# Another order of the input products and other ranks in a planned hybrid encoder block

## The chip, the cores and the metric

The kernel runs on one core of a Trainium2 chip. Its time is the device time of one execution in microseconds (us), the median over several runs; lower is better. The engines that count here are TensorE (PE, with its weight loads PEld), VectorE (DVE), ScalarE (ACT), GpSimd (POOL) and the queue from which all transfers are issued (SP). TensorE's products are the bulk of the work.

## The reference, cut to what matters

One encoder block over 1024 positions of width 1024, eight heads of 128, everything in float32:

```python
h = rms_norm(x, g_mix)
proj = h @ w_in          # glu_a, glu_b | q, k, v | z | decay and beta logits | gate_a, gate_b
c = glu_a * sigmoid(glu_b)
c = depthwise_conv(c, conv_dw_w) + conv_dw_b            # 31 taps
y_conv = silu(layer_norm(c)) @ w_conv_out
q, k, v = silu(depthwise_conv([q, k, v], qkv_conv_w))   # 5 taps, then q and k to unit length
o = rms_norm(gated_delta_rule(q, k, v, ...) + reversed one) * silu(z)
y_delta = o @ w_delta_out
x = x + (sigmoid(gate_a) * y_conv + sigmoid(gate_b) * y_delta) @ w_o
...                                     # SwiGLU, the per-layer embedding, the last norm
```

The change touches the time in which the first four groups of lines are computed, a little over the first half of the run.

## The kernel before, in words

**Products.** A float32 product is made of three products of rounded parts: `mm3` multiplies a high and a low part of the weights with a high and a low part of the activations. One block of 128 output columns needs 24 such products over 512 positions for each half of the positions (in the profile `ps<-big,w 128x512`, called *big products* here). Its weights come by DMA (`raw`), are rounded to the high part on ACT (a cast, `w<-raw`) and subtracted to the low part on DVE (`w<-raw,w`).

**The blocks.** `MAIN` and `FILL` list the blocks of the input projection by a letter and a number: `q`, `k`, `v` (with a 5-tap convolution and SiLU, head by head), `l` (the logits), `g` (a GLU pair, followed on DVE by the 31 taps of its convolution, `conv31`), `z` (the output gate), `a` and `b` (the two branch gates), `p` (the projection of the per-layer input). After them come `conv_out` (the layer norm, named `ln` below, and the product `cout` with `w_conv_out`), and four calls of `group`, the delta rule for two heads each. Later come `dout` (the product with `w_delta_out`, from the stored outputs `d_o` of the heads) and everything else.

**The delta rule.** For two heads, `group` turns k and q (`transpose`, with squares on ACT for their lengths), loads decay rows from DRAM (`big<-dg`) to which ACT adds a bias eight times, forms matrices, and inverts 32 by 32 blocks on DVE (30 pairs of small operations). `head` then joins blocks to 64 and to 128 (`d.lev`: a product `ps<-big`, a negating copy on ACT to a tile `m`, a product `ps<-big,m`, copies of its result on ACT, two STREAM_TRANSPOSE on DVE, and the same once more), and walks along eight chunks in both directions (`d.chain`: products with the state `S`, with `xin` from DVE, with `z2` from ACT). One head follows the other, and other products fill the gaps.

**The order.** Nothing is issued in the order of the code. `Plan` records all operations, and `order` places them by a list schedule with costs of its own: each operation has a rank and a number in the order of recording, and of those that are ready the lowest pair goes first. Tiles are handed out in the order of recording for each line of use.

```python
o.key = (self.level, o.idx)                     # add: rank, then order of recording
pn.level = LV["w"] if 1 <= lv < 3 else lv       # load_w: weights go ahead of their block
if c.key[0] > o.key[0] + 0.6 or ...             # order, on ACT: no table switch for a near rank
w[1][0] < o.key[0] - 0.5                        # order, on DVE: hold a long operation back
```

`LV` holds the ranks: `w` weights, `delta` the delta rule, `qkv`, `glu`, `z` the blocks, `conv31` the taps, `gate` the branch gates, `ln` and `cout` the end of the convolution branch. What follows (`dout` and later) has rank 1. The order is fixed when the kernel is built; on the chip each engine takes its own list in order and waits where an input is late.

Of the kernel before, what the change touches and what calls it, by code (L numbers as in the profile page):

```python
# [565 lines left out]
def cs(j):  # L566
# [2 lines left out]


N_BIG, N_MID, N_W, N_D = 32, 8, 6, 11
LV = dict(w=-3.0, logits=-0.2, delta=-1.8, qkv=1.3, glu=1.2, z=0.5, conv31=2.7, gate=2.3, pl=-0.3, ln=2.1, cout=2.4)
CAP = dict(raw5=6, acc5=3, cpad=10, acc31=1, lnev=3, wmain=4, wfill=2, bank=2, x0=4)
LEAD = (1, 3, 3)
PAIRS = (3, 3, 3)
# [18 lines left out]

MAIN = ("k0 q0 v0 l0 g0 z0 k1 q1 z2 v1 g1 z1 q3 k2 g2 v3 v2 q2 k3 k4 q4 z3 z4 a4 k5 g3 v5 z6 v4 g4 "
        "v6 q5 k7 q6 a5 g5 a7 k6 z5 z7 g6 v7 g7 a6 q7")
FILL = "a0 a2 a3 a1 b0 b1 b2 b3 p0 b4 b5 b6 b7"
PL_AFTER = 2  # L600


def ORDER(f):
# [3 lines left out]
          "a": lambda i: f["do_gate"](0, i), "b": lambda i: f["do_gate"](1, i)}  # L607
    for w in (MAIN + " " + FILL).split():
        do[w[0]](int(w[1:]))
# [5 lines left out]
def hybrid_block(tc, x, p, g_mix, w_in, conv_dw_w, conv_dw_b,  # L615
# [13 lines left out]
    def to(level, stream, sec=None):  # L629
        pn.level, pn.stream, pn.sec = level, stream, sec or stream  # L630

    def large(shape=None, dtype=F32, line="t", cap=99):
        return big.tile(shape or [P, T], dtype, tag="big", line=line, cap=cap)

    def medium(shape=None, dtype=F32, line="ev", cap=4, stream=None):
        return mid.tile(shape or [P, HW], dtype, tag="mid", line=line, cap=cap, stream=stream)
# [65 lines left out]
    def load_w(w, r0, nk, c0, cap=4, pool=None):  # L702

        lv, parts = pn.level, []
        st = "main" if pn.stream == "main" else "rest"
        pn.level = LV["w"] if 1 <= lv < 3 else lv
        for k0 in range(0, nk, 4):
# [135 lines left out]
    def logits():  # L843
        to(LV["logits"], "logits")
        wr = medium([P, KB, 32], line="wab")
# [47 lines left out]
    def load_cols(c0, cap=CAP["wmain"]):  # L893
        return load_w(w_in[0], 0, KB, c0, cap)
# [17 lines left out]
    def do_qkv(which, hd):  # L912
        to(LV["qkv"], "main", "qkv")
        b = which * NH + hd
        w = first_w.pop() if first_w else load_cols(C_Q + b * P)
        raw = large([P, T + SK - 1], line="raw5", cap=CAP["raw5"])
        for h in range(2):
            ps = block_half(w, hA, h, KB)
            pn.act(raw[:, 2 + h * HW:2 + (h + 1) * HW], ps)
        pn.fill(raw[:, 0:2], 0.0)  # L920
        pn.fill(raw[:, T + 2:T + 4], 0.0)
        acc = large(line="acc5", cap=CAP["acc5"])
        conv(acc, raw, cw5[:, b], SK)
        pn.act(acc, acc, AF.Silu)
        pn.dma(d_qkv[which][hd], acc)
# [3 lines left out]
    def do_glu(b):  # L929
        to(LV["glu"], "main", "glu")  # L930
        wb = load_cols(C_GLUB + b * P)
        sg = [ev2(), ev2()]
        for h in range(2):
            pn.act(sg[h], block_half(wb, hA, h, KB), AF.Sigmoid)
        wa = load_cols(C_GLUA + b * P)
        c = large([P, T + CK - 1], line="cpad", cap=CAP["cpad"])
        for h in range(2):
            pa = block_half(wa, hA, h, KB)
            pn.tt(c[:, 15 + h * HW:15 + (h + 1) * HW], pa, sg[h], ALU.mult)
        pn.fill(c[:, 0:15], 0.0)  # L940
        pn.fill(c[:, T + 15:T + 30], 0.0)
        to(LV["conv31"], "conv31")
        acc = large(line="acc31", cap=CAP["acc31"])
        conv(acc, c, cw31[:, b], CK, bias=col["cb31"][:, b:b + 1])
        for h in range(2):
            pn.dma(d_y[b][h], acc[:, hs(h)])
        if b == 0:
            pn.copy(lnacc, acc)
        else:
            pn.tt(lnacc, lnacc, acc, ALU.add)  # L950

    def do_gate(i, b):
        to(LV["gate"], "fill", "gate")
        w = load_cols((C_GA, C_GB)[i] + b * P, CAP["wfill"])
        for h in range(2):
            ps = block_half(w, hA, h, KB)
            sg = ev2()
            pn.act(sg, ps)
            pn.dma(d_gate[i][b][h], sg)
# [954 lines left out]
```

## Time and profile before

| | |
|---|---|
| median of 3 runs | 2108.96 us (2108.37 to 2110.83) |
| the profiled execution: its own time | 2112.86 us |
| its span, first to last instruction | 2111.1 us |
| PE busy | 2071.5 us, 98% |
| DVE busy | 1639.3 us, 78% |
| ACT busy | 1143.8 us, 54% |
| mean granted TensorE clock | 0.994 |

PE is the engine to read: it is nearly always busy, so that the time is what its instructions take, plus the moments in which it waits for another engine or a transfer, plus what a lower granted clock adds. Idle time of DVE or ACT costs nothing by itself. "Who waited for whom" is listed by releaser: an instruction that waits for several things is put down to the last one.

### The profile page before, as it was taken

Reading aid. Unit: us, or ns where it says so; the run is one execution under the profiler, and the core shown is the slowest. Engines: PE = TensorE matmul, PEld = TensorE weight load, DVE = VectorE, ACT = ScalarE, POOL = GpSimd, SP = SyncE. Lnnn points to the kernel's source line nnn. Section 1 sums busy time; section 2 is a strip of 40 time slices with the busy share of each in tenths; the row PEclk is TensorE's granted clock in tenths of the full one; section 3 lists DMA queues with packets and bytes.
Section 4 is the critical chain, followed back from the end, with each engine's and each line's share of the span. In section 5 each row is a group of like instructions: output and inputs, shape, how many; then the busy total and the mean of one; then the engine's idle time right before and its main releaser. Section 6 shows DMA issues by size and latency. Waiting matters only on the chain.

```text
span 2111.1 us, 29502 instructions
## 1 busy us (share of the span) xinstructions
PE 2071.5 (98%) x10279; PEld 1701.3 (81%) x10279; DVE 1639.3 (78%) x2683; ACT 1143.8 (54%) x2603; POOL 129.1 (6%) x197
## 2 busy tenths in 40 slices
PE   8999999999999999999999999999999999999998
PEld 6888888788888788878877788887777777777888
DVE  5578969877999899996687767787666657888776
ACT  6726674657766664857875444433333335443542
POOL 1000111011200211001100000000000000000000
PEclk9999999999999999999999999999999999999999
DMA  6334332533333421544567686433333337442253
GB/s 220 126 102 134 106 118 68 179 95 111 135 101 115 140 83 68 199 149 161 165 206 234 204 278 209 127 120 105 100 96 104 100 99 264 154 160 80 66 161 104
DMA packets 296726, 292.85 MB, mean 139 GB/s; under 512 B 17945, under 2 KB 217810, under 8 KB 296576
## 3 DMA queue, kind: packets, MB, share of 16 engines
q1 hardware_dynamic: 296576, 290.95, 42.8%
q8 instruction: 81, 1.33, 0.3%
q14 instruction: 69, 0.57, 0.1%
HBM read 205.10 MB, written 85.79 MB: 138 GB/s over the span
## 4 chain that ended last, share of the span: by engine, by line
PE 64%; DVE 6%; ACT 4%; issue 1%; DMA 1%; POOL 0%; DVEq 0%; SPq 0%; POOLq 0%; ACTq 0%
PE ps L243 63%; DVE big L291 4%; ACT big L268 2%; PE ps L248 1%; DVE mid L291 1%; DVE w L291 1%; ACT big L275 1%; ACT w L268 0%; ACT m L275 0%; DMA raw<-in_w_delta_out_dram 0%; ACT mid L268 0%; POOL rn L320 0%; DMA mid<-d 0%; DMA big<-dqkv 0%; DMA big<-dg 0%
## 5 line engine op out<-in xcount | busy, mean ns | idle before, releaser
L243 PE MATMUL ps<-big,w 128*128 128x512 f32 (+1 forms) x7416 | 1825.7, 400 | 5.7 <-ACT w L268 3.9
L243 PEld LDWEIGHTS ps<-big,w 128*128 128x128 f32 x7416 | 1360.2, 189 | 316.6 <-ACT w L268 5.8
L291 DVE SCALAR_TENSOR_TENSOR big<-big,cw 128x1024 f32<-128x1024 f32 x336 | 433.5, 1295 | 17.3 <-ACT big L275 11.2
L268 ACT CAST w<-raw 128x512 fp32r<-128x512 f32 (+2 forms) x308 | 185.5, 607 | 275.0 <-PE ps L243 225.8
L291 DVE TENSOR_TENSOR w<-raw,w 128x512 fp32r<-128x512 f32 (+2 forms) x308 | 208.9, 681 | 85.9 <-ACT w L268 83.1
L268 ACT CAST w<-mid 128x512 fp32r<-128x512 f32 (+1 forms) x185 | 108.3, 588 | 153.6 <-PE ps L243 121.9
L291 DVE TENSOR_TENSOR big<-big 128x512 fp32r<-128x512 f32 (+2 forms) x238 | 161.5, 702 | 12.0 <-ACT big L268 8.4
L291 DVE TENSOR_TENSOR w<-mid,w 128x512 fp32r<-128x512 f32 (+1 forms) x185 | 118.7, 644 | 60.3 <-ACT w L268 59.4
L291 DVE TENSOR_TENSOR big<-ps,big 128x512 f32<-128x512 f32 (+1 forms) x146 | 99.9, 687 | 36.6 <-PE ps L243 27.2
L268 ACT CAST big<-big 128x512 fp32r<-128x512 f32 x163 | 96.2, 622 | 43.7 <-DVE big L291 23.3
L268 ACT COPY big<-big 32x128 f32<-32x128 f32 (+1 forms) x264 | 103.1, 441 | 18.7 <-DVE big L291 16.8
L243 PE MATMUL ps<-big 128*128 128x128 f32 (+1 forms) x784 | 104.6, 280 | 7.8 <-ACT big L268 5.1
L243 PEld LDWEIGHTS ps<-big 128*128 128x128 f32 x784 | 98.9, 191 | 16.4 <-issue 11.2
L268 ACT COPY big<-ps 128x512 f32<-128x512 f32 (+3 forms) x178 | 74.9, 429 | 65.3 <-PE ps L243 56.2
L275 ACT ACTIVATE mid<-mid 128x512 f32<-128x512 f32 (+2 forms) x87 | 50.4, 584 | 51.9 <-DVE mid L291 28.4
L243 PEld LDWEIGHTS ps<-S,big 128*128 128x128 f32 x448 | 69.2, 190 | 11.4 <-DVE S L291 2.9
L243 PE MATMUL ps<-S,big 128*128 128x128 f32 x448 | 74.9, 276 | 0.6 <-DVE S L291 0.6
L268 ACT COPY m<-ps 128x512 f32<-128x512 f32 x52 | 30.4, 587 | 76.8 <-PE ps L243 76.7
L268 ACT COPY mid<-ps 128x512 f32<-128x512 f32 x71 | 41.1, 585 | 55.5 <-PE ps L243 45.7
L248 PE MATMUL ps<-ident,big 128*128 128x128 f32 (+2 forms) x368 | 61.1, 280 | 9.9 <-DMA big<-in_x_dram 4.9
L243 PEld LDWEIGHTS ps<-big,m 128*128 128x128 f32 x512 | 62.6, 194 | 7.6 <-ACT m L275 5.3
L275 ACT ACTIVATE big<-big 128x1024 f32<-128x1024 f32 (+2 forms) x80 | 56.7, 718 | 22.0 <-DVE big L291 18.6
(161 smaller groups left out, 1717.6 us busy)
## 6 DMA issues: line engine op xcount, KB each, us to landing
raw<-in_w_in_dram SPq DMA_DIRECT2D x128, 256.0 KB, 3.1
mid<-d SPq DMA_DIRECT2D x120, 256.0 KB, 3.6
d<-big SPq DMA_DIRECT2D x119, 256.0 KB, 3.0
big<-d SPq DMA_DIRECT2D x119, 256.0 KB, 5.1
d<-mid SPq DMA_DIRECT2D x100, 256.0 KB, 2.1
big<-dqkv SPq DMA_DIRECT2D x32, 512.0 KB, 5.1
raw<-in_w_gate_up_dram SPq DMA_DIRECT2D x50, 256.0 KB, 3.1
dqkv<-big SPq DMA_DIRECT2D x24, 512.0 KB, 2.6
```

The costliest lines, as they stand in the source:

```text
L243: o = self.add("pe", lambda: self.nc.tensor.matmul(out.ap(), lhsT.ap(), rhs.ap(), start=start, stop=stop, **kw), [out], [lhsT, rhs], cost)
L248: self.add("pe", lambda: self.nc.tensor.transpose(out.ap(), in_.ap(), ident.ap()), [out], [in_, ident], 0.11)
L268: return self.nc.scalar.copy(out.ap(), in_.ap())
L275: return self.nc.scalar.activation(out.ap(), in_.ap(), func, **kw)
L291: return getattr(e, name)(**{k: v.ap() if isinstance(v, View) else v for k, v in kw.items()})
```

## The change

Three tables of constants are edited; no function is. In `MAIN`, `g2` goes ahead of `q3`, and the following blocks of heads 2 and 3 are taken in another order. In `FILL`, `b7` goes ahead of `b5` and `b6`. Three ranks move: `delta` from -1.8 to -1.65, `conv31` from 2.7 to 3, `gate` from 2.3 to 2.45 (`w` stays -3).

```diff
-LV = dict(w=-3.0, logits=-0.2, delta=-1.8, qkv=1.3, glu=1.2, z=0.5, conv31=2.7, gate=2.3, pl=-0.3, ln=2.1, cout=2.4)
+LV = dict(w=-3, logits=-0.2, delta=-1.65, qkv=1.3, glu=1.2, z=0.5, conv31=3, gate=2.45, pl=-0.3, ln=2.1, cout=2.4)
-MAIN = ("k0 q0 v0 l0 g0 z0 k1 q1 z2 v1 g1 z1 q3 k2 g2 v3 v2 q2 k3 k4 q4 z3 z4 a4 k5 g3 v5 z6 v4 g4 "
+MAIN = ("k0 q0 v0 l0 g0 z0 k1 q1 z2 v1 g1 z1 g2 q3 v2 k2 q2 v3 k3 k4 q4 z3 z4 a4 k5 g3 v5 z6 v4 g4 v6 q5 "
...
```

By the order alone, only two of the edits move instructions: the new `MAIN`, from block `g2` on, and the rank of `gate`, which now stands behind `cout` (2.4) instead of ahead of it. The other two ranks pass no other rank and no distance that the rules above compare, and `b7` ahead of `b5` and `b6` exchanges three blocks of equal shape. All engines have the same instructions as before, in another order, from about 225 us to about 1200 us. Three places show what moved.

The first place is on PE and on DVE, at the start of `d.lev` of the last head (head 8; `big` are its block matrices, `m` the negated product). Before, on PE from the transposes that end head 7, and on DVE from the products with head 7's norm `rn`:

```order
L248 MATMUL ps<-ident,m_9952 128x128 x4
L243 MATMUL ps<-big,w 128x512
L243 MATMUL ps<-big 128x128 x4
L243 MATMUL ps<-big,w 128x512 x6
L243 MATMUL ps<-big,m_9991 128x128 x4
L243 MATMUL ps<-big,w 128x512 x5
L243 MATMUL ps<-big 128x128 x4
```

```order
L291 TENSOR_TENSOR m_9952<-big,rn 128x512
L291 TENSOR_TENSOR w<-raw,w 128x512
L291 SCALAR_TENSOR_TENSOR mid<-ps,vec_t,mid 128x512 x2
L291 STREAM_TRANSPOSE big<-big 32x4x32
L291 TENSOR_TENSOR w<-raw,w 128x512 x2
L291 STREAM_TRANSPOSE big<-big 32x4x32
```

The same two stretches with the change:

```order
L248 MATMUL ps<-ident,m_9707 128x128 x4
L243 MATMUL ps<-big 128x128 x4
L243 MATMUL ps<-big,w 128x512 x4
L243 MATMUL ps<-big,m_9737 128x128 x4
L243 MATMUL ps<-big,w 128x512 x9
L243 MATMUL ps<-big 128x128 x4
```

```order
L291 TENSOR_TENSOR m_9700<-big,rn 128x512
L291 TENSOR_TENSOR m_9707<-big,rn 128x512
L291 SCALAR_TENSOR_TENSOR mid<-ps,vec_t,mid 128x512 x2
L291 STREAM_TRANSPOSE big<-big 32x4x32 x2
L291 TENSOR_TENSOR big<-big,mid 128x512
```

Between the product with `m` and the next product with the block matrices stand nine big products instead of five, and the two weight subtractions between the two transposes on DVE are gone from there.

The second place is on PE, in `d.lev` of heads 7 and 8, where column sums (a product with `ones`, one column wide) of the convolution branch and of the per-layer input are taken. Before, in head 7:

```order
L243 MATMUL ps<-big 128x128 x4
L243 MATMUL ps<-big,w 128x512
L243 MATMUL ps<-ones,big 128x1 x5
L243 MATMUL ps<-big,m_9378 128x128 x4
L243 MATMUL ps<-ones,big 128x1 x9
L243 MATMUL ps<-big 128x128 x4
L243 MATMUL ps<-ones,big 128x1 x2
L243 MATMUL ps<-big,w 128x512 x2
```

With the change eight of the sixteen sums stand earlier, in the chain of head 7 among big products, and the others in head 8:

```order
L243 MATMUL ps<-big,w 128x512 x6
L243 MATMUL ps<-ones,big 128x1 x2
L243 MATMUL ps<-big,m_9787 128x128 x4
L243 MATMUL ps<-big 128x128 x4
L243 MATMUL ps<-ones,big 128x1 x6
L243 MATMUL ps<-big,m_9828 128x128 x4
L243 MATMUL ps<-big,w 128x512 x8
```

The sixteen sums with twelve narrow products around them are now two shorter stretches.

The third place is on SP, where `dout` is about to start: the first pieces of `w_delta_out` (`raw`), the last stored head outputs (`big<-d`) and the last pieces of `w_conv_out`. Before:

```order
L340 DMA mid<-d_2840 128x512
L340 DMA raw<-in_w_conv_out_dram 128x4x128
L340 DMA big<-d_7447 128x512
L340 DMA raw<-in_w_conv_out_dram 128x4x128
L340 DMA big<-d_8116 128x512
L340 DMA raw<-in_w_delta_out_dram 128x4x128 x2
L340 DMA big<-d_7459 128x512
```

With the change:

```order
L340 DMA mid<-d_4070 128x512
L340 DMA raw<-in_w_conv_out_dram 128x4x128
L340 DMA raw<-in_w_delta_out_dram 128x4x128
L340 DMA big<-d_7410 128x512
L340 DMA big<-d_8079 128x512
L340 DMA raw<-in_w_delta_out_dram 128x4x128 x2
L340 DMA d_11274<-mid 128x512
```

The first piece of `w_delta_out` now goes out ahead of the two head outputs instead of behind them, and one piece of `w_conv_out` has gone out earlier.

More of the change, by code (lines that the diff above doesn't have):

```diff
@@ L592 @@
 GU_MARK = 10
-MAIN = ("k0 q0 v0 l0 g0 z0 k1 q1 z2 v1 g1 z1 q3 k2 g2 v3 v2 q2 k3 k4 q4 z3 z4 a4 k5 g3 v5 z6 v4 g4 "
-        "v6 q5 k7 q6 a5 g5 a7 k6 z5 z7 g6 v7 g7 a6 q7")
-FILL = "a0 a2 a3 a1 b0 b1 b2 b3 p0 b4 b5 b6 b7"
+MAIN = ("k0 q0 v0 l0 g0 z0 k1 q1 z2 v1 g1 z1 g2 q3 v2 k2 q2 v3 k3 k4 q4 z3 z4 a4 k5 g3 v5 z6 v4 g4 v6 q5 "
+        "k7 q6 a5 g5 a7 k6 z5 z7 g6 v7 g7 a6 q7")
+FILL = "a0 a2 a3 a1 b0 b1 b2 b3 p0 b4 b7 b5 b6"
 PL_AFTER = 2
```

## The prediction

> **What bounds the kernel now.** I read the page's head first, then the busy time by stage, then who PE waited for in the stretch that the change reorders.
>
> ```profile
> span 2111.1 us, 29502 instructions
> PE 2071.5 (98%) x10279; PEld 1701.3 (81%) x10279; DVE 1639.3 (78%) x2683; ACT 1143.8 (54%) x2603; POOL 129.1 (6%) x197
> ```
>
> ```profile
> core 0: us, PE busy (x) PEld busy (x) DVE busy (x) ACT busy (x) POOL busy (x), PEclk, DMA share, GB/s
> 51.00:200.00 149.00, 148.91 (x696) 121.50 (x695) 108.98 (x163) 83.98 (x190) 3.61 (x11) 1.00 0.38 123
> 200.00:950.00 750.00, 738.39 (x4004) 617.46 (x4003) 659.94 (x1052) 474.92 (x1281) 90.57 (x131) 1.00 0.37 119
> 950.00:1050.00 100.00, 96.17 (x594) 83.79 (x593) 64.50 (x118) 80.90 (x222) 16.68 (x22) 0.97 0.50 159
> 1050.00:1200.00 150.00, 142.55 (x665) 114.95 (x664) 121.21 (x213) 95.24 (x182) 3.01 (x2) 0.98 0.67 210
> ```
>
> ```profile
> PE ps L243 <- ACT big L268: 5.1, 4, 1.7
> PE ps L243 <- ACT w L268: 3.9, 3, 3.0
> PE ps L243 <- DVE big L291: 2.8, 2, 2.4
> PE ps L243 <- DVE xin L291: 2.7, 4, 0.9
> PE ps L248 <- ACT ps L275: 2.6, 2, 2.2
> PE ps L243 <- DVE lnb L291: 1.8, 1, 1.8
> PE ps L248 <- DVE m L291: 1.4, 3, 0.7
> PE ps L243 <- ACT z L275: 0.7, 1, 0.7
> PE ps L243 <- ACT m L268: 0.7, 1, 0.7
> PE ps L243 <- DVE S L291: 0.6, 1, 0.6
> ...
> ```
>
> PE bounds every stage. The list (total us, times, longest) covers 50 to 1200 us; its rows shown sum to 22.3 us, against 22.98 us of idle in the four slices (149 + 750 + 100 + 150 less the busy 148.91 + 738.39 + 96.17 + 142.55). PE's instructions are the same before and after, so the change can only move these waits and the moments of lower clock. Waits plus the clock losses worked out below (6.5 us) give at most 29 us to win; nothing in the profile limits what could be lost. DVE is busy 88% from 200 to 950 us (659.94 of 750), so it is the engine that a bad order would make late.
>
> **The change, part by part.**
>
> *Edits at nothing.* `delta`, `conv31` and `FILL` move no instruction: 0.
>
> *The start of head 8's level products.* This is the 2.4 us wait on DVE:
>
> ```profile
> 1022.71 1.41 PE L243 MATMUL ps<-big,w 128*128 128x512 f32 x5
> 1024.13 0.30 DVE L291 STREAM_TRANSPOSE big<-big 32x128 f32<-32x128 f32 x1 [3.17 <-PE ps L243]
> 1024.77 1.29 DVE L291 TENSOR_TENSOR w<-raw,w 128x512 fp32r<-128x512 f32 x2 [0.34 <-ACT w L268]
> 1026.10 0.31 DVE L291 STREAM_TRANSPOSE big<-big 32x128 f32<-32x128 f32 x1
> 1026.55 1.22 PE L243 MATMUL ps<-big 128*128 128x128 f32 x8 [2.43 <-DVE big L291]
> 217.60 5.73 PE L243 MATMUL ps<-big,w 128*128 128x512 f32 x24
> ```
>
> The five big products are over, and the last transpose stands behind two weight subtractions (1.29 us). The change puts nine products there; in a dense run 24 take 5.73 us, 0.239 us each, so four more cover 0.96 us. The two subtractions leave: 1.29 us. Together 2.25 of 2.43 us: **-2.2**, between -2.43 and 0 (something else is late in their place).
>
> *Clock drops.* Slices cut to the moments at which the granted clock changes (start and end, length, PE's busy time, granted clock, DMA share, GB/s):
>
> ```profile
> 968.80:972.80 4.00, 4.00 (x38) 1.00 0.83 225
> 972.80:976.20 3.40, 3.40 (x15) 0.51 0.91 345
> 1024.00:1027.40 3.40, 0.97 (x8) 1.00 0.16 48
> 1027.40:1030.80 3.40, 3.40 (x11) 0.51 0.62 193
> 1146.90:1150.30 3.40, 1.09 (x5) 1.00 0.78 229
> 1150.30:1153.70 3.40, 2.74 (x6) 0.51 0.53 173
> 1153.70:1157.10 3.40, 3.40 (x9) 0.50 0.86 243
> 969.62 2.07 PE L243 MATMUL ps<-ones,big 128*128 128x1 f32 x18
> ```
>
> A slice at half clock does half its work. The drop at 1027.4 follows a slice in which PE was busy 0.97 of 3.40 us, the wait above; it cost 3.40 x 0.5 = 1.7 us and goes with it: **-1.7** (0 if it stays). The drop at 972.8 follows a slice without idle, but full of one-column sums: 18 passes, two per sum, in 2.07 us. With the change the narrow stretch in head 8 has eight sums and twelve narrow products, twenty at 0.23 us (2.07 / 9), 4.6 us; half of its products are no sums. It can still fill a slice of 3.4 us, but with fewer sums: of 1.7 us I take **-1.2**, between -1.7 and 0.
>
> [...]
>
> *The start of `dout`.* The longest wait (3.0 on ACT's cast of weights):
>
> ```profile
> 1142.88 5.97 DMA raw<-in_w_delta_out_dram
> 1150.96 24.82 PE L243 MATMUL ps<-big,w 128*128 128x512 f32 x91 [2.97 <-ACT w L268]
> ```
>
> The chain of waits leads from PE through the cast to the first piece of `w_delta_out`, which took 5.97 us behind other transfers. The change sends it ahead of two head outputs, 0.26 MB each (128 x 512 x 4 bytes). At the 229 GB/s of the slice from 1146.9 the 0.52 MB take 2.3 us: **-2.3** of 2.97. Ends: -2.97, and +1 if head outputs, now later, become what `dout` needs last. With 0.7 us of wait in place of 2.97 the slice before would be busy at least 2.7 of 3.4 us, and the two slices at half clock go: their busy 2.74 + 3.40 us at 0.5 is **-3.1**, or 0.
>
> *The end of head 8's chain.* `z` and `S` waited 0.7 and 0.6 us among casts for `cout`; `cout` now starts later, with gates there instead, which need casts too: half, **-0.6**, from -1.3 to 0.
>
> *Decay rows.* PE waits where ACT's eight biases stand ahead of squares that PE's transposes need, and the row is late:
>
> ```profile
> 390.95 2.44 ACT L275 ACTIVATE big<-big,gneg 128x128 f32<-128x128 f32 x8 [2.49 <-DMA big<-dg]
> 393.73 0.33 PE L248 MATMUL ps<-ident,big 128*128 128x128 f32 x1 [2.20 <-ACT ps L275]
> ```
>
> Only two of eight heads paid for it (2.6 us in all). The rows are reloaded in another neighbourhood for heads 3 to 8, with the same pattern on ACT: 0, from -2.6 to +4.4 (two more heads at 2.20).
>
> *New waits.* In head 7 a product with `m` follows its source by two big products where there were four: 0.48 us less cover, +0.5. Everything else between 230 and 1200 us is a new order too. The waits of no named place (`xin` 2.7, `m` 1.4, `big` on ACT 5.1, `lnb` 1.8) make 11 us over the eight heads and the norm; I expect them again at about that sum, and a fifth more, **+2.0**, for places that were covered and no longer are, from -3 (a fourth fewer) to +6 (half as many again).
>
> Sum: -2.2 - 1.7 - 1.2 - 2.3 - 3.1 - 0.6 + 0.5 + 2.0 = -8.6 us. The profiled execution (2112.86 us, span 2111.1, 1.8 us around it) was 3.9 us over the median of its runs; a difference worked out in it is carried to the median: 2108.96 - 8.6 = **2100.4 us**.
>
> **The rivals.**
>
> 1. *The end of the stretch keeps its waits.* The DMA engines are busy 0.78 and 0.86 in the slices around 1150 us; what is sent first there only makes another transfer late, and `dout` waits for a head output or its parts instead. Then -2.3 and -3.1 fall away: -3.2, 2105.8 us; with new waits at +4 instead of +2, 2107.8. For it: a busy queue. Against: the chain names that one piece, and nothing in front of it needs it less.
>
> 2. *Slower: DVE falls behind in heads 2 and 3.* `g2` comes earlier, so its 30 taps start while head 2 walks its chain.
>
> ```profile
> 229.00:262.00 33.00, 33.00 (x193) 27.97 (x192) 32.15 (x37) 22.69 (x59) 5.03 (x8) 1.00 0.42 139
> 296.00:328.00 32.00, 31.66 (x186) 26.58 (x186) 16.36 (x24) 22.57 (x57) 5.58 (x10) 1.00 0.44 149
> 495.20 10.08 DVE L291 SCALAR_TENSOR_TENSOR big<-big,cw 128x1024 f32<-128x1024 f32 x7
> 505.20 0.60 DVE L291 SCALAR_TENSOR_TENSOR xin<-ps,e_ng,big 128x128 f32<-128x128 f32 x2
> ```
>
> DVE has 15.6 us free in head 2's chain (32 - 16.36) and each tap takes 1.44 us (10.08 / 7); an `xin` behind one is late, as at 505.20, at 0.68 us a time (2.7 / 4). Heads 2 and 3 have 28 such steps: all late is 19 us, 2119.5 us. It decides from 19 of the 28 (8.6 + 4.2 over 0.68). Against it: head 1's chain (229 to 262) had DVE busy 32.15 of 33 and PE without a gap.
>
> 3. *The drops of the clock stay,* wherever narrow products and waits meet a slice: +2.9 on the sum, 2103.3 us.
>
> 4. *More goes than I count:* the waits of the short kind thin out too (-3 instead of +2) and all named ones vanish: -16, 2093 us.
>
> **How the numbers follow.** The forecast as summed has 0.45, rival 1 0.26, rival 2 0.14, rival 3 0.10, rival 4 0.05. About 0.2%, 4.2 us, is what a measurement of this kernel tells from no change. Faster by more, under 2104.7: forecast, 3, 4, and a little of rival 1 (0.02): 0.62. Within: most of rival 1 (0.22) and the mild part of rival 2 (0.03): 0.25. Slower: the rest of 2 and 0.02 of 1, 0.13. The range from 2092 to 2109.5 leaves out the slow end of rival 2 and little at the low end; the forecast's own, from its terms' ends, is 2094 to 2104.
>
> **What would show it.** The wait on DVE at head 8's transposes gone, PE's slice there full; no half clock at these three places, or only one; the first `dout` product waiting under 1 us; everything after 1200 us the same. Wrong it is if `dout` waits as long for another tile, if several heads wait on decay rows (PE on ACT's `ps`, over 5 us), or if `xin` waits rise past 10 us in heads 2 and 3.

## The result, and the profile after

| | before | changed |
|---|---|---|
| median beside each other | 2109.66 us (4 runs, 2108.37 to 2110.83) | 2097.34 us (4 runs, 2093.55 to 2098.82) |
| ratio | | 0.9939, 95% interval 0.9922 to 0.9956 |
| the same beside the experiments | 2109.91 us (15 runs) | 2094.98 us (5 runs), ratio 0.9934 (0.9921 to 0.9947) |
| profiled execution: its time, its span | 2112.86 us, 2111.1 us | 2098.03 us, 2096.3 us |

The change makes the kernel 12 to 15 us faster; the forecast was 8.6. First the page's head, the four stretches and the list of waits from 50 to 1200 us, as they were shown of before:

```profile
span 2096.3 us, 29498 instructions
PE 2062.6 (98%) x10279; PEld 1696.6 (81%) x10279; DVE 1640.2 (78%) x2683; ACT 1144.8 (55%) x2603; POOL 129.7 (6%) x197
```

```profile
core 0: us, PE busy (x) PEld busy (x) DVE busy (x) ACT busy (x) POOL busy (x), PEclk, DMA share, GB/s
51.00:200.00 149.00, 148.95 (x697) 121.55 (x696) 109.17 (x164) 84.06 (x190) 3.61 (x11) 1.00 0.38 123
200.00:950.00 750.00, 736.42 (x4041) 617.40 (x4039) 667.23 (x1056) 486.42 (x1316) 94.75 (x138) 1.00 0.37 118
950.00:1050.00 100.00, 98.95 (x644) 88.01 (x645) 70.24 (x151) 82.59 (x230) 15.19 (x16) 1.00 0.47 152
1050.00:1200.00 150.00, 147.50 (x637) 117.75 (x636) 119.71 (x193) 89.48 (x147) 1.01 (x1) 1.00 0.77 243
```

```profile
PE ps L243 <- ACT big L268: 5.3, 3, 2.4
PE ps L248 <- ACT ps L275: 3.2, 3, 2.1
PE ps L243 <- DVE xin L291: 2.3, 4, 0.8
PE ps L243 <- ACT w L268: 1.8, 2, 1.1
PE ps L243 <- ACT mid L268: 1.4, 1, 1.4
PE ps L248 <- DVE m L291: 1.2, 2, 0.8
PE ps L243 <- ACT m L268: 0.7, 1, 0.7
PE ps L243 <- ACT m L275: 0.6, 2, 0.4
PE ps L243 <- DVE S L291: 0.2, 1, 0.2
```

The idle time of PE in the four stretches is 17.2 us (1149 less the busy 1131.82) where it was 23.0. The granted clock is 1.00 in all of them; before it was 0.97 and 0.98 in the last two. From 200 to 950 us, where most instructions were moved, PE is no busier than before (736.42 against 738.39 us). The gain lies behind 950 us. In the list of waits, `DVE big` (2.8), `DVE lnb` (1.8) and `ACT z` (0.7) are gone, and the weights' casts (`ACT w`) fell from 3.9 to 1.8. Of the 14.8 us between the two spans, 5.8 are idle time, 6.5 are the four slices at half clock that before had between 60 and 2080 us and this execution has not (12.94 us of busy PE in them, reckoned at half speed). The row of big products in the fourth comes out a little faster than half: ten took 4.41 us from 1152.95 us, 0.441 each, where a dense run at clock 1.00 takes 0.239 each; at that rate the four slices are 5.9 us. The other 2.5 to 3.1 us are not idle time: they lie in PE's busy time, whose ends the profile models, and nothing here shows their cause.

The three places, in the timeline of PE (start, us, what, idle before it). The start of head 8's level products, the column sums in head 7's chain, then the start of `dout`:

```profile
989.11 1.14 PE L243 MATMUL ps<-big,m 128*128 128x128 f32 x8
990.01 2.34 PE L243 MATMUL ps<-big,w 128*128 128x512 f32 x9
992.18 1.05 PE L243 MATMUL ps<-big 128*128 128x128 f32 x8
947.47 1.40 PE L243 MATMUL ps<-ones,big 128*128 128x1 f32 x12
950.23 0.68 PE L243 MATMUL ps<-z,big 128*128 128x128 f32 x4 [1.36 <-ACT mid L268]
1141.45 8.23 PE L243 MATMUL ps<-big,w 128*128 128x512 f32 x34 [0.78 <-ACT w L268]
1150.73 13.26 PE L243 MATMUL ps<-big,w 128*128 128x512 f32 x55 [1.05 <-ACT w L268]
```

Head 8's level products wait for nothing. The sums stand apart, though a wait of 1.36 us, for a copy on ACT, has come behind them. `dout` waits 0.78 us for its first weights instead of 2.97, and has a second wait of 1.05 us that it did not have.

### The profile page after: what moved, and what is told of

Its sections match the earlier page's. It is cut to its first block, busy times and chain, and to the rows that moved or that the text cites. A ratio compares the mean times of both kernels' runs of the same rounds, so it can differ in the third digit from the quotient of the medians.

```text
span 2096.3 us, 29498 instructions
## 1 busy us (share of the span) xinstructions
PE 2062.6 (98%) x10279; PEld 1696.6 (81%) x10279; DVE 1640.2 (78%) x2683; ACT 1144.8 (55%) x2603; POOL 129.7 (6%) x197
## 4 chain that ended last, share of the span: by engine, by line
PE 59%; DVE 7%; issue 6%; ACT 4%; DMA 2%; POOL 1%; SPq 0%; DVEq 0%; POOLq 0%; ACTq 0%
PE ps L243 58%; DVE big L291 5%; ACT big L268 2%; DVE mid L291 1%; DVE w L291 1%; PE ps L248 1%; DMA big<-d 1%; DMA mid<-d 1%; ACT big L275 1%; POOL rn L320 0%; ACT m L275 0%; ACT w L268 0%; ACT ps L275 0%; ACT mid L275 0%; DMA big<-dg 0%
## 5 line engine op out<-in xcount | busy, mean ns | idle before, releaser
L275 ACT ACTIVATE mid<-mid 128x512 f32<-128x512 f32 (+2 forms) x87 | 50.5, 584 | 50.6 <-DVE mid L291 30.6
L291 DVE TENSOR_TENSOR big<-big,mid 128x512 f32<-128x512 f32 (+11 forms) x158 | 61.9, 392 | 13.0 <-ACT mid L275 8.4
```

What stands on the lines that cost most here:

```text
L275: return self.nc.scalar.activation(out.ap(), in_.ap(), func, **kw)
L291: return getattr(e, name)(**{k: v.ap() if isinstance(v, View) else v for k, v in kw.items()})
```

## The experiments

All but the last four start from the kernel before. Ratios are to the kernel before, on the same chip. Single runs of one kernel lie up to 15 us apart here (2102.01 to 2116.73 us with the rank alone); the fourth group shows a good part of the reason. So the medians and the intervals count, and a profile shows one execution of its kernel.

### Each edit alone

```diff
-... z1 q3 k2 g2 v3 v2 q2 k3 k4 ...      # e1_main: MAIN as in the change, gate stays
+... z1 g2 q3 v2 k2 q2 v3 k3 k4 ...
-gate=2.3                                # e2_gate: the rank alone
+gate=2.45
```

> The kernel before with the new MAIN alone (gate stays at 2.3). Theory: the gains at head 8 and at the column sums come from MAIN, the gain at the start of dout from the rank of gate. So the DVE wait at head 8 (2.43 us) and the half clocks at 972.8 and 1027.4 (1.7 us each) go, dout still waits about 3 us for its first weights and its half clock (3.1 us) stays: about 6 to 8 us below the kernel before (near 2102.5 us), four to six above the changed kernel. Rival A, it is all MAIN: 2097 to 2098 us, dout waits under 1 us. Rival B, it is all gate: no difference (2108 to 2110 us), the wait at head 8 stays.

> The kernel before with the rank of gate alone (2.45). The order is the one before until about 1020 us. Theory: dout's first wait falls from 2.97 to about 0.8 us and its half clock (3.1 us) goes; the half clock at 972.8 stays, the wait at head 8 stays at 1 to 2.4 us: about 4 to 6 us below the kernel before (near 2104.5 us). Rival A, all MAIN: no difference (2108 to 2110 us) with dout waiting as before. Rival B, all gate: 2097 to 2098 us.

Measured: `MAIN` alone 2103.55 us, ratio 0.9974 (0.9965 to 0.9983); the rank alone 2109.75 us, 0.9998 (0.9986 to 1.0009). The timeline of PE at `dout`, `MAIN` alone first, then the rank alone:

```profile
1139.35 0.73 PE L243 MATMUL ps<-big,w 128*128 128x512 f32 x2 [1.42 <-ACT w L268]
1153.58 2.79 PE L243 MATMUL ps<-big,w 128*128 128x512 f32 x6 [4.32 <-ACT w L268]
```

```profile
1147.84 6.15 PE L243 MATMUL ps<-big,w 128*128 128x512 f32 x25 [3.17 <-ACT w L268]
1171.78 1.06 PE L243 MATMUL ps<-big,w 128*128 128x512 f32 x3 [1.70 <-DVE big L291]
```

`MAIN` did what the theory gave it: head 8's wait and the two clock drops around it are gone (from 950 to 1050 us PE is busy 99.70 us, at a clock of 1.00). For the rank the theory failed: alone it leaves `dout` waiting 3.17 us and adds waits behind. With `MAIN` it is worth another 6 to 9 us (2103.55 to 2097.34 or 2094.98), because with `MAIN` alone `dout` has a second wait of 4.32 us. The two edits do not add up: -6.5 and -0.3 apart, -12 to -15 together.

### One wait taken away where it stands

In the next runs, operations of the finished order are put behind a named one; everything else keeps its place. First the transposes of head 8. In `e7_level` DVE goes from the first of these to the second (ACT alike, with its two casts; each engine's other work and the order on PE and SP stay):

```diff
-STREAM_TRANSPOSE big<-big | TENSOR_TENSOR w<-raw,w x2 | STREAM_TRANSPOSE big<-big
+STREAM_TRANSPOSE big<-big x2 | TENSOR_TENSOR w<-raw,w x2
```

> The kernel before with one move alone, at head 8's level product: the two casts on ACT and the two weight subtractions on DVE that stood between the two STREAM_TRANSPOSE are put behind the second one; PE and SP keep their order of before. Theory: the wait of 2.43 us falls to about 1.1 us, PE's slice there is two thirds busy, and the half clock at 1027.4 (1.7 us) goes: 2.5 to 3.5 us below the kernel before (near 2106.5 us), with the half clocks at 972.8 and 1150.3 kept. Rival A: the half clock has another cause than the wait and stays: 1 to 1.5 us below. Rival B: the moved casts are late for the next products and give the gain back: no difference.

Measured: 2110.25 us, ratio 0.9997 (0.9986 to 1.0008), no gain. PE at the place, and ACT in front of the second wait:

```profile
1021.91 1.13 PE L243 MATMUL ps<-big 128*128 128x128 f32 x8 [0.80 <-DVE big L291]
1026.38 1.16 PE L243 MATMUL ps<-big,m 128*128 128x128 f32 x8 [1.47 <-ACT m L275]
```

```profile
1022.09 1.14 ACT L268 CAST w<-raw 128x512 fp32r<-128x512 f32 x2
1023.26 1.08 ACT L268 COPY lnb<-ps 128x512 f32<-128x512 f32 x2
1024.22 1.09 ACT L268 COPY mid<-ps 128x512 f32<-128x512 f32 x2
1025.17 0.65 ACT L268 CAST w<-raw 128x512 fp32r<-128x512 f32 x1
1025.69 0.63 ACT L275 ACTIVATE m<-ps 128x512 f32<-128x512 f32 x1
```

The wait fell from 2.43 to 0.80 us, and 1.47 us came back at the next product of the same chain: its negating copy `m` stands on ACT behind the casts that were pushed back and what had queued behind them. Rival B was right in the sum, at another tile than it named. In the change the first transposes are covered by nine big products, and on ACT one weight cast stands in front of that negating copy (at 993.49 us) instead of three casts and four copies.

At `dout`, the exchange on SP (`e6_piece`), then with it the weights' casts on ACT ahead of the head outputs' (`e11_both`), then the casts alone (`e12_casts`):

```diff
-raw<-w_conv_out | big<-d | raw<-w_conv_out | big<-d | raw<-w_delta_out    # SP: e6, e11
+raw<-w_conv_out x2 | raw<-w_delta_out | big<-d | big<-d
-CAST w | CAST big x2 | CAST w | CAST big | CAST w | CAST big x6          # ACT: e11, e12
+CAST w x3 | CAST big x9
```

> The kernel before with one exchange on SP alone: the first piece of w_delta_out is sent ahead of the two head outputs that were sent ahead of it; every other engine has its order of before. Theory (the prediction's step): dout's first wait falls by up to 2.3 us from 2.97, PE's slice before it is fuller, and the half clock of 6.83 us behind it (3.1 us) goes: 2104 to 2105 us. Rival A: the piece lands about 1 us earlier, as its issue does, since the transfer's 5.97 us do not depend on the two in front of it: dout waits near 2 us, the half clock stays in part: 2107 to 2109 us. Rival B: dout waits as long for a head output: no difference.

> The kernel before, at the start of dout alone: the exchange on SP of the run with one piece sent earlier, and besides the first two weight casts on ACT (and their subtractions on DVE) put ahead of the casts of the head outputs that stood in front of them. Theory: the weights were held by the order on ACT behind head outputs, not by their transfer; with both moved the first wait falls from 3 to 4.4 us to about 1.5 us, about 1 us comes back where the head outputs are now late, and PE's slices there stay over half busy, so that no half clock follows: 2 to 5 us below the kernel before (2105 to 2108 us). Rival A: the weights' transfer ends last anyway: first wait stays over 2.5 us, no difference. Rival B: the head outputs, cast later, take the whole gain back in a second wait: no difference in time, first wait short.

> As the run before it without the exchange on SP: only the casts and subtractions of the first two weights go ahead of the head outputs. Theory: the first piece, sent 1 us later behind two head outputs, now ends last: the first wait is 1 to 2 us longer than with both, 2.5 to 3.5 us, and a half clock follows in part of the runs: 0 to 3 us below the kernel before (2107 to 2110 us). Rival (the transfer does not matter at all): the same as with both moved.

Measured: 2109.79 us, 1.0003 (0.9994 to 1.0011); 2109.32 us, 0.9998 (0.9989 to 1.0007); 2110.89 us, 1.001 (1.0002 to 1.0019). With the exchange on SP alone, PE (one row) and ACT:

```profile
1147.11 5.26 PE L243 MATMUL ps<-big,w 128*128 128x512 f32 x12 [4.41 <-ACT w L268]
1144.88 0.62 ACT L268 CAST big<-big 128x512 fp32r<-128x512 f32 x1 [0.58 <-DVE big L291]
1145.40 0.61 ACT L268 CAST w<-raw 128x512 fp32r<-128x512 f32 x1
1146.44 0.61 ACT L268 CAST w<-raw 128x512 fp32r<-128x512 f32 x1
```

The piece was issued at 1138.98 us, and the six pieces of weights issued around it landed within 4.6 us each, this one by 1143.6. By the kernel's order on ACT the cast at 1145.40 is that of the last piece of `w_conv_out`; this piece's own is the one at 1146.44, in a row without a gap behind a cast of a head output that waited for DVE. So the order on ACT held the weights, not the transfer that the chain of waits had named. The profile of before has the same row of casts:

```profile
1148.73 0.62 ACT L268 CAST big<-big 128x512 fp32r<-128x512 f32 x1 [0.58 <-DVE big L291]
1150.29 0.61 ACT L268 CAST w<-raw 128x512 fp32r<-128x512 f32 x1
```

There the piece had landed at 1148.85 us (1142.88 + 5.97), 1.44 us ahead of its cast at 1150.29. With both moved, PE reads:

```profile
1144.59 0.74 PE L243 MATMUL ps<-big,w 128*128 128x512 f32 x2 [0.53 <-ACT w L268]
1145.92 1.19 PE L243 MATMUL ps<-big,w 128*128 128x512 f32 x4 [0.59 <-DVE w L291]
1147.70 0.49 PE L243 MATMUL ps<-big,w 128*128 128x512 f32 x1 [0.58 <-ACT big L268]
1156.43 0.73 PE L243 MATMUL ps<-big,w 128*128 128x512 f32 x2 [1.61 <-ACT w L268]
```

The first wait is short (0.53), and the rest comes back in pieces, for the low part, a head output, and the next weights. The casts alone made it no better either (2.21 us first, 1.07 later). Weights, head outputs, ACT and DVE are all late there by about the same time. That something else ends the wait instead was the prediction's first rival, and for these local edits it holds, though the profiles name ACT and DVE for it, not a busy queue.

### Another block moved

`e8_g2` moves one block of `MAIN` that the change also moves; `e9_g4`, the control, one that it does not.

```diff
-... z1 q3 k2 g2 v3 ...      # e8_g2
+... z1 g2 q3 k2 v3 ...
-... z6 v4 g4 v6 ...         # e9_g4
+... z6 g4 v4 v6 ...
```

> The kernel before with one block of MAIN moved: g2 ahead of q3, and nothing else. Theory: heads 2 and 3, where the block moves, wait as before (229 to 480 us: within 1.5 us); what changes is how the places at 920 to 1180 us fall, since the whole order behind the block is another. By this order the sums stand apart (913 to 928 us of PE's work, in six groups) and dout starts with two products and cout between, as in the changed kernel: 4 to 10 us below the kernel before (2100 to 2106 us). Rival A, the gain belongs to the new order of heads 2 and 3: 3 us or more less wait between 229 and 480 us. Rival B (the prediction's second): xin waits in heads 2 and 3, over 5 us there, slower than before.

> A control: the kernel before with another block moved by one place, g4 ahead of v4 in MAIN, where the change moves nothing; gate stays at 2.3. The order is the one before until about 500 us. Theory: the order of before had three places that happened to be late, and another order of the same length is likely better; at dout this one has PE's order of the changed kernel (two products, two of cout, seven, twenty-three of cout), so dout's waits should be near its 3 us and not 5.8, while head 8's level product has four big products of cover instead of nine: 3 to 8 us below the kernel before (2102 to 2107 us). Rival (the gain is tied to what the change moves): 2108 to 2111 us, dout and head 8 wait as before.

Measured: 2100.93 us, ratio 0.9959 (0.9946 to 0.9973), and 2110.66 us, 1.0003 (0.9995 to 1.0012). Heads 2 and 3 (229 to 480 us), with `g2` moved and then before:

```profile
229.00:480.00 251.00, 249.07 (x1356) 207.99 (x1355) 204.67 (x329) 163.28 (x431) 29.08 (x49) 1.00 0.36 115
229.00:480.00 251.00, 246.51 (x1329) 205.93 (x1328) 206.52 (x329) 156.59 (x417) 28.33 (x48) 1.00 0.36 116
```

`g2` alone is worth 9 us, no less than all of `MAIN` (6.5; the intervals overlap). Part of it, 2.6 us, does lie in heads 2 and 3, contrary to the theory's 1.5; in the changed kernel this part is not there (its PE is busy 245.08 of the 251 us). The prediction's second rival is refuted: DVE did not fall behind (`xin` waits of 0.6 us in all from 50 to 1200 us here, 2.3 in the changed kernel). The control gained nothing. At `dout` it has PE's order of the changed kernel and still waits:

```profile
1152.80 23.36 PE L243 MATMUL ps<-big,w 128*128 128x512 f32 x89 [3.53 <-ACT w L268]
```

In it the first piece of `w_delta_out` went out at 1146.19 us, 3.1 us before PE ran dry; in the changed kernel at 1134.48 us, 6.2 us before. Both times it stood in the queue behind the store of a finished `cout` block (`d<-mid`), for which SP waited. From that store to the first product after the wait both take about the same, 8.0 us (1144.78 to 1152.80) and 8.4 us (1133.06 to 1141.45). So in these two profiles it is how far the other engines are ahead of PE that decides, not PE's order at the place. Why the changed kernel is 3 us further ahead there was not isolated.

One number ranks these orders before anything runs: the length that the list schedule itself arrives at (`self.length`, set by `order`). Computed from the kernels of these runs it is 2093.6 us before, and shorter by 0.4 us for the rank alone and for the control, by 3.7 for `MAIN` alone, by 5.7 for `g2` alone and by 8.9 for the change. On the chip the first two make no difference, and the others follow in the same order: 6.5, 9.0, and 12 to 15 us. The schedule's costs leave out these drops of the clock, which the next group prices at 4.2 us for the change; 8.9 + 4.2 makes 13.1.

### The half clock

Two runs on the changed kernel: each of the sixteen one-column sums issued three times (`e4_thrice`), and the same 64 columns wide (`e5_thrice_wide`).

```diff
-pn.matmul(ps[:, i:i + 1], acc[:, cs(i)], ones[:, 0:1], True, True)
+pn.matmul(ps[:, i:i + 1], acc[:, cs(i)], ones[:, 0:1], True, True)               # x3: e4
+pn.matmul(ps[:, 64 * i:64 * i + 64], acc[:, cs(i)], ones[:, 0:64], True, True)   # x3: e5
```

> The changed kernel with each of the sixteen one-column sums issued three times: 32 more on PE at about 0.223 us, 7.1 us, in the two places (head 7's chain, head 8's level products); all else in the same order. Theory: what halves the clock behind a busy PE is that a whole slice of 3.41 us holds little but one-column products; 24 sums in a row (5.4 us) fill at least one slice at each place, however the slices lie: one or two half clocks come back, +1.7 us each beside the 7.1: 2106 to 2109 us, with half clock in the trace near 950 or 1000 us. Rival: only idle time of PE halves the clock: 2104 to 2105 us and no half clock there.

> As the run before it, but the repeated sums are 64 columns wide instead of one (same count, same places; a product this short takes PE the same 0.223 us). Theory: the slices then hold 64 times the columns and the clock stays: 2104 to 2105 us, 1.7 to 3.4 us below the run with one-column sums. Rival A (idle time alone): both the same, no half clock in either. Rival B: 64 columns are still too few: both the same, with half clocks in both.

Measured: 2107.59 us, ratio 0.9985 (0.9975 to 0.9995), and 2103.65 us, 0.9974 (0.9964 to 0.9984). Slices at the sums, one column wide and then 64 (PE's busy time is the second figure, the granted clock the third from the end):

```profile
946.56:949.97 3.41, 3.41 (x33) 3.41 (x32) 0.69 (x1) 1.99 (x6) 0.00 (x0) 1.00 0.91 345
949.97:953.38 3.41, 3.41 (x15) 3.12 (x15) 0.50 (x2) 1.83 (x5) 1.61 (x4) 0.50 0.16 46
```

```profile
945.11:948.52 3.41, 3.41 (x30) 3.28 (x29) 0.69 (x1) 3.16 (x11) 0.40 (x1) 1.00 0.85 268
948.52:951.93 3.41, 3.41 (x33) 3.41 (x32) 0.29 (x2) 0.57 (x3) 0.26 (x2) 1.00 0.85 313
```

PE is without a gap in all four. Behind the slice of 33 one-column products the clock is half (0.50). Behind those of 64 columns it is not: it is 1.00 in the second of these slices, and three big products behind it take 0.94 us (at 951.86), as three ahead of the sums do (at 945.13). The wide kernel is 3.9 us faster in the median, with a mean clock of 0.9964 over its runs against 0.9945 (0.0019 x 2100 = 4.0 us). The intervals of the ratios overlap, and the two profiled executions took the same time (2102.13 and 2102.45 us), so the medians alone would not carry it; the slices do. Idle time of PE cannot be all that matters: it was busy for the whole 3.41 us ahead of this half clock.

In the execution before, half clock began at 972.84, 1027.46 and 1150.34 us and lasted 3.42, 3.41 and 6.82 us. Some slices with one-column products or with waits, and the clock in the 3.41 us behind each:

| run, slice in us | PE busy in it | passes | clock behind it |
|---|---|---|---|
| before, 969.43 to 972.84 | 3.41 us | 34, of them 22 one column wide | 0.50 |
| `e4_thrice`, 946.56 to 949.97 | 3.41 us | 33, all one column wide | 0.50 |
| `e4_thrice`, 997.75 to 1001.16 | 3.41 us | 34, of them some 18 one column wide (36 took 4.08 us from 999.16) | 1.00 |
| before, 1024.05 to 1027.46 | 0.98 us | 10 | 0.50 |
| before, 1146.93 to 1150.34 | 1.06 us | 5 | 0.50 |
| `e1_main`, 1150.36 to 1153.78 | 0.20 us | 1 | 0.50 |
| `e1_main`, 1146.95 to 1150.36 | 2.31 us | 10 | 1.00 |
| after, 1140.30 to 1143.70 | 2.62 us | 12 | 1.00 |

Half clock stands behind two kinds of slices in the table: with PE busy 0.20 to 1.06 us, or busy all the time with 22 of 34 and 33 of 33 passes one column wide. These are single slices, and what the clock goes by was not shown.

The kernel with the rank alone has the order of before up to about 1020 us, the sums included. In its profiled execution PE is busy and the clock 1.00 all through them (961.92 to 975.57 us), where that of before drops at 972.84: one and the same order got half clock there in one execution and not in another. Drops that come and go account for a good part of the spread of the runs. Over 82 runs of the kernel before, the mean granted clock was 0.9948; those at 0.994 took 2111.2 us in the mean, those at 0.996 2107.8. The changed kernel has 0.9968 over nine runs, which is 0.0020 x 2100 = 4.2 us.

### The changed kernel once more, and with its own waits moved

`e10_local` puts fourteen groups of operations of the changed order elsewhere, as above; `e13_after` is the changed kernel itself.

> The changed kernel with 14 local moves on ACT and DVE at its longest remaining waits, PE's order unchanged: at three decay rows the two squares go ahead of the eight biases; weight casts that stood amid the block copies go behind them (heads 1, 3, 5); one convolution tap goes behind xin (three places) or behind the product with rn (three places); some layer norm steps behind it (head 8); one cast of a head output behind the first weights of dout. Theory: each takes away what it names, 2.2 + 0.7 + 0.8 at the decay rows, 0.6 + 0.6 + 1.2 at the copies, 0.6 + 1.0 + 0.9 at xin, 0.3 + 0.3 + 0.5 + 1.0 at the products with rn, 0.5 at dout, 11 us in all, of which two thirds or more stay won: 2087 to 2091 us, 6 to 10 below the changed kernel. Rival: the next operation in the same chain is as late each time (as in the run with head 8's transposes, where 1.6 of 2.4 us came back at the next product): 2094 to 2097 us.

> The changed kernel once more, beside the others on the same chip, since single runs of one kernel differ by up to 8 us here and the result has four. Expected 2096 to 2098.5 us, and if half clocks that come and go with the run are what spreads the runs, a mean clock that falls as the time rises, by about 2.1 us for 0.001, and a lower spread than the kernel before.

Measured: 2096.15 us with local moves (5 runs, ratio 0.9942, 0.9929 to 0.9954), 2094.98 us without (0.9934, 0.9921 to 0.9947): no gain. With local moves, the longest rows of the list of waits, and one place on PE, then DVE in front of it:

```profile
PE ps L248 <- DVE m L291: 4.2, 5, 1.5
PE ps L243 <- ACT big L268: 2.4, 2, 1.4
1047.59 0.66 PE L248 MATMUL ps<-ident,m 128*128 128x128 f32 x4 [1.52 <-DVE m L291]
```

```profile
1044.43 0.69 DVE L291 TENSOR_TENSOR m<-big,rn 128x512 f32<-128x512 f32 x1 [1.75 <-POOL rn L320]
1045.04 0.69 DVE L291 TENSOR_TENSOR mid<-mid,lnb 128x512 f32<-128x512 f32 x1
1045.64 0.68 DVE L291 TENSOR_TENSOR w<-raw,w 128x512 fp32r<-128x512 f32 x1
1046.25 0.69 DVE L291 TENSOR_TENSOR big<-mid,big 128x512 fp32r<-128x512 f32 x1
1046.85 0.69 DVE L291 TENSOR_TENSOR m<-big,rn 128x512 f32<-128x512 f32 x1
```

What was put behind the first product with `rn` now stood in front of the second, and the wait came there (1.52 us where 0.8 had been). Waits for ACT's `big` fell from 5.3 to 2.4 us and decay rows from 3.2 to 0.8, `m` rose from 1.2 to 4.2 (and ACT's `m`, L275, from 0.6 to 1.7). The moves won at their places and lost one step on: the list sums to 13.3 us, and so does that of the second profile of the changed kernel. No version beat the changed kernel.

In the second profile of the changed kernel PE's idle time in the four stretches is 13.9 us, not 17.2, and `dout`'s first wait is 0: such figures hold to about 3 us from one execution to the next. Over its five runs the mean clock fell from 0.998 (2092.8 us) to 0.995 (2099.8): 2.3 us for 0.001, near the 2.1 expected. Its runs spread over 7.0 us, the kernel before over 10.5 in fifteen runs, which says little.

## Why the prediction was right, and where its steps were not

The direction and the range held; the sum came out 3.7 us short of the result (6.3 short of the second measurement). The waits gave more than forecast and the clock less, so that the sum is nearer than its parts; that nearness is luck.

- *Edits at nothing.* Right by the order: with `delta`, `conv31` or `FILL` alone changed, `order` gives each engine the list that it had, but for the exchange of equal blocks. None of them was run alone. What failed is that the prediction gave each place its price as if places were independent; `MAIN` and `gate` are worth more together than apart.
- *Head 8's level products, -2.2.* The whole 2.43 us went. The split was wrong: the two subtractions were credited with 1.29 us, and taking them away alone moved 1.47 us to the next product. What remains of the step is the cover by nine big products; that it alone would do was not run.
- *Clock drops, -1.7, -1.2, -3.1.* Between the two profiles that the result gives, all of them went, 6.5 us where 6.0 were forecast, both reckoned at half speed (5.9 us at the 0.441 us of a big product there). Over the runs the clock gives 4.2. The step that failed is the one that carries a difference of one execution to the median: this execution stood 3.9 us above its median, and part of that were drops that other runs did not have (its mean clock was 0.994, that of the 82 runs 0.9948, which is 0.0008 x 2100 = 1.7 us).
- *The sums.* No half clock came. At the sums of head 8, from 993.40 to 1000.20 us, PE is busy throughout at a clock of 1.00, with 6 and 12 one-column passes among the 28 of each half; the slice of before had 22 of 34. That fits the reason given, few sums in a slice, but how many it takes was not shown.
- *The start of `dout`, -2.3.* The first wait fell by 2.2 us, but the step's cause is refuted: sending the piece earlier, alone, won nothing, and in the profile of before it had landed 1.44 us ahead of its cast. The chain of waits was read as if the cast had waited for the transfer, where ACT was held by the casts in front. A second wait of 1.05 us is the head outputs' and next weights' turn, as the first rival had it; the rest of the gain needs `MAIN` and the rank together.
- *The end of head 8's chain, -0.6.* All of the 1.3 us went; the 0.2 us for `S` in the list after the change stand in another head (728.68 us).
- *Decay rows, 0.* From 2.6 to 3.2 us; near enough. *Head 7's `m`, +0.5:* it came, 0.39 us at 933.32 us.
- *New waits, +2.0.* This is the term most wrongly sized. What had no named place did not recur in full: `lnb` 1.8 us went altogether, `xin` went from 2.7 to 2.3, `big` on ACT from 5.1 to 5.3, and the one large newcomer is `mid`, 1.4. The named rows sum to 16.7 us against 22.3, 5.6 less, where the sum had 2.6 less.

So waits gave 3.0 us more than forecast in the first profile and over 6 in the second, and the clock 1.8 less than forecast over the runs. Rival 1 would have left 2105.8 us or more and `dout` waiting; it did not come for the change as a whole. Rival 2 is refuted (its 2119.5 us is 2119.4 by its own terms), rival 3 only in part (drops do return in some executions: of the changed kernel's nine runs two have a mean clock of 0.995, three 0.998), rival 4's direction was the right one.

## What to carry to other kernels

A wait's named releaser is often one of several that are late by the same time (at `dout` 2.97 us on one of them before; with two moved 0.53, 0.59 and 0.58 us on three); count a wait as gain only if the next operations of the same chain on the same engines come earlier too. Price a moment of low clock by the chance that it happens, over the runs' mean clocks, not by the one execution that shows it. When a planner orders everything, an edit's worth lies far from the edit, and two edits do not add: compare whole orders, by the planner's own length first (it ranked these six rightly), then on the chip.

## What was not expected of the hardware

The clock halved with PE busy all the time: behind 3.41 us in which 22 of 34 passes were one column wide (the kernel before, 969.43 to 972.84 us), and behind one of 33 such passes (`e4_thrice`, 946.56 to 949.97 us). With passes of 64 columns in their place (`e5_thrice_wide`) it stayed at 1.00. It also halved behind slices with waits, where PE was busy 0.20, 0.98 and 1.06 us of 3.41. A single drop of the kernel before lasted 3.41 or 3.42 us; at 0.441 us for a big product in place of 0.239 that is an estimated 1.6 us lost. One and the same order got a drop at the sums in one execution (before, at 972.84 us) and none in another (the rank alone, 1.00 from 961.92 to 975.57 us).
